# Gate and up as seven block products, 256 tokens moving, outputs through DRAM

## The chip, the core and the metric

The kernel runs on one core of a Trainium2 chip. The metric is device microseconds of one execution; less is better. The engines are TensorE (PE, its weight loads shown apart as PEld), VectorE (DVE), ScalarE (ACT), GpSimd (POOL) and SyncE (SP, which here only issues DMAs).

## The reference, cut to what matters

One decoder block over 512 tokens, D = 2048, in fp32. The change is in its last part, the feed-forward with 5632 hidden columns:

```
u = rmsnorm(h) * (1 + scale2) + shift2                    # 512 x 2048
h = h + gate2 * ((silu(u @ w_gate) * (u @ w_up)) @ w_down)
return rmsnorm(h) * final_norm
```

w_gate and w_up are 2048 x 5632, w_down is 5632 x 2048.

## The kernel before

Activations lie transposed: a tile holds 128 features by 512 tokens. To keep fp32 accuracy at the speed of the fp32r type, every operand is split in a high and a low part (fp32r each) and a product is three matmuls: high*high, low*high, high*low. `mm_ws` (L252 to L255) issues the three with the weights stationary (128x128) and 512 tokens moving; `mm_as` (L257 to L260) does it with activations stationary and up to 288 weight columns moving.

`gemm` walks over the contraction in pairs of 128 rows. For each pair `load_w` brings 128x2x512 weights from DRAM (512 KB, SP queue), ACT casts them to the high part `wh` (L237), DVE subtracts to get the low part `wl` (L238), and PE does 2 x 4 x 3 = 24 matmuls.

The feed-forward runs in four phases over the hidden columns (3, 3, 3 and 2 groups of 512). In a phase each group does a gemm for gate (16 x 4 x 3 = 192 matmuls), SiLU on ACT from PSUM, a gemm for up, the product on DVE (L1045), and the split of the result into `fh`, `fl` (L1048, L1049), which stay in SBUF; then four gemms of `w_down` over the phase's hidden columns, added into `hT` (L999). Over the four phases gate and up are 4224 matmuls and down is 2112, all 512 wide.

Ahead of it the sixteen tiles of `hT` are summed in squares (`sum_rstd`, L819), spread over the partitions (`rows_of`, L171, copied by ACT at L173), and `modulate` makes the sixteen pairs `uh`, `ul` (L384, L386, L390). The last sixth of the adaLN vector is summed on the side (`ada_block`, L356). SP's queue stands in the order in which the code issues; the other engines' order here comes from a scheduler.

## Time and profile before

| | us |
|---|---|
| median of 3 runs | 2519.36 |
| lowest, highest | 2513.86, 2526.12 |
| span of the profiled execution | 2530.7 |
| PE busy in it | 2408.5 (95%) |
| DVE, ACT, POOL busy | 1253.7, 775.3, 231.9 |

Only the profiled execution has a span per instruction; it is 11.3 us longer than the median of the runs that were timed without being shown in detail. Below, a row of a timeline gives start, duration, engine, line, operation, output and inputs; a matmul's duration overlaps the next one's start, so that the pitch is the difference of two starts.

### The profile page before, as it was taken

To read this page: it belongs to the slowest core of one execution; us is meant where nothing else is said; L and a number is where in the kernel's file an instruction comes from. 1 tells how busy PE (TensorE), PEld (TensorE's weight loads), DVE (VectorE), ACT (ScalarE), POOL (GpSimd) and SP (SyncE) were. 2 spreads that over 40 slices of the span, in tenths; PEclk is the share of its full clock that TensorE was granted. 3 is DMA by queue.
4 is the path that set the end of the run, shared out by engine and by line. 5 is a ranking of instruction groups with operands and counts; after the bars stand their busy time and mean duration, and the time that the engine had idled before them with its cause. 6 is when DMAs were issued, how large, how long until landed. Compare 5 with 4: busy or idle time off the path is not lost.

```text
span 2530.7 us, 29434 instructions
## 1 busy us (share of the span) xinstructions
PE 2408.5 (95%) x11475; PEld 2005.5 (79%) x11475; DVE 1253.7 (50%) x1978; ACT 775.3 (31%) x1221; POOL 231.9 (9%) x204
## 2 busy tenths in 40 slices
...
GB/s 301 226 275 77 187 151 125 124 156 114 189 149 150 86 206 226 149 175 191 159 100 92 100 96 96 100 94 97 100 92 100 98 93 100 96 96 100 93 99 100
DMA packets 226794, 339.02 MB, mean 134 GB/s; under 512 B 17648, under 2 KB 102480, under 8 KB 226656
## 3 DMA queue, kind: packets, MB, share of 16 engines
...
q14 instruction: 48, 0.39, 0.1%
...
## 4 chain that ended last, share of the span: by engine, by line
PE 60%; DMA 2%; DVE 1%; issue 0%; ACT 0%; SPq 0%; POOLq 0%; POOL 0%; ACTq 0%; DVEq 0%
PE psmm L253 10%; PE psmm L255 10%; PE psmm L254 10%; PE pss L255 7%; PE pss L253 7%; PE pss L254 7%; PE pso L254 2%; PE pso L253 2%; PE pso L255 2%; DMA wr<-in_w_out_dram 1%; DMA ad<-in_w_ada_dram 1%; DVE acc L356 0%; DVE wl L238 0%; PE psmm L819 0%; ACT wh L237 0%
## 5 line engine op out<-in xcount | busy, mean ns | idle before, releaser
L238 DVE TENSOR_TENSOR wl<-wr,wh 128x1024 fp32r<-128x1024 f32 (+2 forms) x370 | 433.6, 1172 | 966.7 <-ACT wh L237 965.1
L237 ACT CAST wh<-wr 128x1024 fp32r<-128x1024 f32 (+2 forms) x386 | 384.5, 996 | 1199.5 <-PE pso L254 521.7
L253 PE MATMUL psmm<-uh,wh 128*128 128x512 f32 x1010 | 401.0, 398 | 11.9 <-ACT uh L386 5.7
L254 PE MATMUL psmm<-ul,wh 128*128 128x512 f32 x1010 | 398.3, 394 | 2.0 <-DVE ul L390 2.0
L255 PE MATMUL psmm<-uh,wl 128*128 128x512 f32 x1010 | 398.4, 395 | 1.3 <-DVE wl L238 1.3
L253 PE MATMUL pss<-uh,wh 128*128 128x512 f32 x600 | 238.9, 398 | 17.8 <-ACT uh L386 17.8
L254 PE MATMUL pss<-ul,wh 128*128 128x512 f32 x600 | 238.5, 398 | 5.2 <-DVE ul L390 5.2
L255 PE MATMUL pss<-uh,wl 128*128 128x512 f32 x600 | 237.9, 397 | 1.0 <-POOL wl L238 0.9
L253 PEld LDWEIGHTS psmm<-uh,wh 128*128 128x128 f32 x1010 | 192.2, 190 | 54.5 <-ACT uh L386 6.8
L356 DVE SCALAR_TENSOR_TENSOR acc<-ad,sl,acc 128x512 f32<-128x512 f32 x240 | 187.7, 782 | 94.8 <-DMA ad<-in_w_ada_dram 92.2
L255 PEld LDWEIGHTS psmm<-uh,wl 128*128 128x128 f32 x1010 | 192.4, 190 | 43.6 <-DVE wl L238 2.4
L254 PEld LDWEIGHTS psmm<-ul,wh 128*128 128x128 f32 x1010 | 192.2, 190 | 41.7 <-DVE ul L390 3.0
L992 POOL TENSOR_TENSOR fsum<-fsum,sq 128x512 f32<-128x512 f32 x13 | 19.4, 1492 | 1452.7 <-ACT sq L990 1452.0
L253 PEld LDWEIGHTS pss<-uh,wh 128*128 128x128 f32 x600 | 115.3, 192 | 43.9 <-ACT uh L386 19.7
L254 PEld LDWEIGHTS pss<-ul,wh 128*128 128x128 f32 x600 | 115.3, 192 | 31.0 <-DVE ul L390 7.0
L253 PE MATMUL psmm<-fh,wh 128*128 128x512 f32 x352 | 136.9, 389 | 0.0
L254 PE MATMUL psmm<-fl,wh 128*128 128x512 f32 x352 | 136.9, 389 | 0.0
L255 PE MATMUL psmm<-fh,wl 128*128 128x512 f32 x352 | 136.9, 389 | 0.0
L255 PEld LDWEIGHTS pss<-uh,wl 128*128 128x128 f32 x600 | 115.2, 192 | 26.0 <-POOL wl L238 1.8
L492 DVE SCALAR_TENSOR_TENSOR acc<-ad,sl,acc 128x256 f32<-128x256 f32 x144 | 111.2, 772 | 4.8 <-DMA ad<-in_w_ada_dram 0.5
L253 PE MATMUL pss<-fh,wh 128*128 128x512 f32 x264 | 102.7, 389 | 0.0
L254 PE MATMUL pss<-fl,wh 128*128 128x512 f32 x264 | 102.7, 389 | 0.0
...
## 6 DMA issues: line engine op xcount, KB each, us to landing
ad<-in_w_ada_dram SPq DMA_DIRECT2D x192, 512.0 KB, 4.4
wr<-in_w_gate_dram SPq DMA_DIRECT2D x88, 512.0 KB, 3.7
wr<-in_w_up_dram SPq DMA_DIRECT2D x88, 512.0 KB, 3.7
wr<-in_w_down_dram SPq DMA_DIRECT2D x88, 512.0 KB, 3.7
wr<-in_w_in_dram SPq DMA_DIRECT2D x104, 256.0 KB, 3.7
wr<-in_w_in_dram SPq DMA_DIRECT2D x24, 512.0 KB, 4.6
wr<-in_w_out_dram SPq DMA_DIRECT2D x24, 512.0 KB, 4.8
...
```

What stands on the lines that cost most here:

```text
L237: nc.scalar.copy(wh[:, :, s], v)
L238: lo.tensor_tensor(wl[:, :, s], v, split_ap(wh)[:, :, s], op=OP.subtract)
L253: nc.tensor.matmul(dst, wh[:, k, w], ah, start=first, stop=False)
L254: nc.tensor.matmul(dst, wh[:, k, w], al, start=False, stop=False)
L255: nc.tensor.matmul(dst, wl[:, k, w], ah, start=False, stop=last)
L356: nc.vector.scalar_tensor_tensor(acc, wr[:, q, :], s, acc, op0=OP.mult, op1=OP.add)
L492: nc.vector.scalar_tensor_tensor(acc, tiles[n][:, q, :], sc1, acc, op0=OP.mult, op1=OP.add)
L992: nc.gpsimd.tensor_tensor(acc[0], acc[0], sq, op=OP.add)
```

## The change

Gate and up are computed together, as one 2x2 block product: the weights' blocks are (up, gate) by the two halves of the contraction, the activations' blocks are the two halves of the contraction by the two halves of the tokens. The product of 2x2 blocks takes seven block products here (P1 to P7) instead of eight, on sums and differences of blocks that are made beforehand: `w_sums` makes four blocks from the four raw weight blocks, `u_mix` four from the activations. A step s is one 128-row slice of each half for 256 hidden columns: 7 x 2 x 3 = 42 matmuls, the weights stationary, 256 tokens moving. Eight steps make a group of 256 hidden columns; there are 22 groups, 176 steps. Each product has a PSUM bank of its own, out of eight; `evac` adds them up into gate and up, `glu` makes the hidden values, and POOL's queue stores them to DRAM (`hd`), from where `h_tile` reads them again for down.

The low parts of the three blocks that are used unsummed are made by ACT (minus the raw block, rounded to fp32r) and a DMA that adds the raw block onto it (`x_low`, POOL's queue); those of the sums by DVE (`s_split`). `hT` is stored to DRAM after the attention part and read back for down. The order of all engines from the modulation to the first four hidden tiles of down is the code's own (`manual_schedule`). Not shown in the diff: the rope tables move to another pool, `ada_load` and `ada_add` (one 128x256 multiply-add on DVE a step for 128 steps).

```diff
+    fs = ExitStack()
+    ring1 = pool(fs, "ring1", side="right", reuse_waits="tile")
...
+    res = pool(rs, "res", side="right", reuse_waits="tile")
...
+    hT = [res.tile([P, T], F32, name=f"hT{i}") for i in range(ND)]
+    hsd = [dram.tile([P, T], F32, name=f"hsd{i}") for i in range(ND)]
...
+    KG, NG, HT = ND // 2, DFF // 256, T // 2
+    S = KG * NG
+    wg_v = w_gate.rearrange("(h k p) n -> p h k n", h=2, p=P)
+    wu_v = w_up.rearrange("(h k p) n -> p h k n", h=2, p=P)
+    hd = [dram.tile([P, 2, T], F32, name=f"hd{g}") for g in range(NG)]
...
+    def w_load(s):
+        g, k = divmod(s, KG)
+        c = slice(g * HT, (g + 1) * HT)
+        raw[s] = ring1.tile([P, 4, HT], F32, tag="raw", name=uid("raw"), bufs=6)
+        nc.sync.dma_start(raw[s][:, 0:2, :], wu_v[:, :, k, c])
+        nc.sync.dma_start(raw[s][:, 2:4, :], wg_v[:, :, k, c])
+    def w_sums(s):
+        f, t = raw[s], ring1.tile([P, 4, HT], F32, tag="sum", name=uid("sum"), bufs=2)
+        nc.vector.tensor_tensor(t[:, 0:2, :], f[:, 1:3, :], f[:, 0:1, :].to_broadcast([P, 2, HT]), op=OP.add)
+        nc.vector.tensor_tensor(t[:, 2, :], t[:, 0, :], f[:, 2, :], op=OP.add)
+        nc.vector.tensor_tensor(t[:, 3, :], t[:, 2, :], f[:, 3, :], op=OP.add)
+        sums[s] = t
+    def x_high(s):
+        hx[s] = ring1.tile([P, 3, HT], F32R, tag="hx", name=uid("hx"), bufs=3)
+        nc.scalar.copy(hx[s], raw[s][:, 1:4, :])
+    def x_low(s):
+        lx[s] = ring2.tile([P, 3, HT], F32R, tag="lx", name=uid("lx"), bufs=4)
+        nc.scalar.activation(lx[s], raw[s][:, 1:4, :], AF.Copy, scale=-1.0)
+        nc.gpsimd.dma_start(split_ap(lx[s]), raw[s][:, 1:4, :], accum_op=OP.add)
+    def s_split(s):
+        hs[s] = ring2.tile([P, 4, HT], F32R, tag="hs", name=uid("hs"), bufs=2)
+        ls[s] = ring2.tile([P, 4, HT], F32R, tag="ls", name=uid("ls"), bufs=2)
+        nc.scalar.copy(hs[s], sums[s])
+        nc.vector.tensor_tensor(ls[s], sums[s], split_ap(hs[s]), op=OP.subtract)
...
+    def u_raw(k):
+        ur[k] = []
+        for i in (k, k + KG):
+            dst = hT[i] if k < 5 else ev.tile([P, T], F32, tag="ev", name=uid("ur"), bufs=6)
+            nc.vector.scalar_tensor_tensor(dst, hT[i], a_vec[:, 1, i:i + 1], rb, op0=OP.mult, op1=OP.mult)
+            ur[k].append(dst.rearrange("p (a b) -> p a b", b=HT))
+    def u_mix(k, eng):
+        a, b = ur[k]
+        t = ring2.tile([P, 4, HT], F32, tag="tmix", name=uid("tmix"), bufs=2)
+        eng.tensor_tensor(t[:, 0, :], a[:, 1, :], a[:, 0, :], op=OP.subtract)
+        eng.tensor_tensor(t[:, 3, :], b[:, 1, :], t[:, 0, :], op=OP.subtract)
+        eng.tensor_tensor(t[:, 2, :], b[:, 1, :], a[:, 1, :], op=OP.subtract)
+        eng.tensor_tensor(t[:, 1, :], t[:, 3, :], b[:, 0, :], op=OP.subtract)
+        tmix[k] = t
+    def u_split(k):
+        a, b = ur.pop(k)
+        t = tmix.pop(k)
+        h, l = (upool[k // 5].tile([P, 7, HT], F32R, tag="u" + c, name=uid("u" + c), bufs=5 if k < 5 else 3)
+                for c in "hl")
+        sa, sb = (mod[:, 3 * ND + i:3 * ND + i + 1] for i in (k, k + KG))
+        for lo, n, v, sh in ((0, 1, a[:, 0:1, :], sa), (1, 2, b, sb), (3, 2, t[:, 0:2, :], None),
+                            (5, 1, t[:, 2:3, :], dsh[:, k:k + 1]), (6, 1, t[:, 3:4, :], sb)):
+            d = slice(lo, lo + n)
+            if sh is None:
+                nc.scalar.copy(h[:, d, :], v)
+                nc.vector.tensor_tensor(l[:, d, :], v, split_ap(h)[:, d, :], op=OP.subtract)
+            else:
+                nc.scalar.activation(h[:, d, :], v, AF.Identity, bias=sh)
+                nc.vector.scalar_tensor_tensor(l[:, d, :], v, sh, split_ap(h)[:, d, :], op0=OP.add, op1=OP.subtract)
+        V[k] = h, l
+    PROD = (("P1", "x", 1, 0), ("P2", "x", 2, 1), ("P6", "s", 2, 6), ("P7", "s", 1, 5), ("P5", "s", 0, 3),
+            ("P3", "s", 3, 2), ("P4", "x", 0, 4))
+    B = {}
+    def pe(s):
+        g, k = divmod(s, KG)
+        vh, vl = V[k]
+        for name, kind, wi, vi in PROD:
+            if k == 0:
+                B[name] = ps2.tile([P, 2, HT], F32, tag="y", name=uid("py"), bufs=8)
+            wh, wl = (hx[s], lx[s]) if kind == "x" else (hs[s], ls[s])
+            for j in range(2):
+                o, js = B[name][:, j, :], slice(j * P, (j + 1) * P)
+                nc.tensor.matmul(o, wh[:, wi, js], vh[:, vi, :], start=k == 0 and j == 0, stop=False,
+                                 skip_group_check=True)
+                nc.tensor.matmul(o, wh[:, wi, js], vl[:, vi, :], start=False, stop=False, skip_group_check=True)
+                nc.tensor.matmul(o, wl[:, wi, js], vh[:, vi, :], start=False, stop=k == KG - 1,
+                                 skip_group_check=True)
+    def ev_tile():
+        return ev.tile([P, 2, HT], F32, tag="ev", name=uid("ev"), bufs=6)
+    def evac(g):
+        g2, g1, u1, u2 = (ev_tile() for _ in range(4))
+        tt = nc.vector.tensor_tensor
+        nc.scalar.copy(g2, B["P1"])
+        tt(g1, g2, B["P2"], op=OP.add)
+        tt(g2, g2, B["P6"], op=OP.subtract)
+        tt(u1, g2, B["P7"], op=OP.add)
+        tt(g2, g2, B["P5"], op=OP.subtract)
+        tt(u2, B["P5"], u1, op=OP.subtract)
+        tt(g2, g2, B["P3"], op=OP.add)
+        tt(u1, u1, B["P4"], op=OP.add)
+        return g, g1, g2, u1, u2
+    def glu(g, g1, g2, u1, u2):
+        nc.scalar.activation(g1, g1, AF.Silu)
+        nc.scalar.activation(g2, g2, AF.Silu)
+        nc.vector.scalar_tensor_tensor(u1, u1, -1.0, g1, op0=OP.mult, op1=OP.mult)
+        nc.vector.tensor_tensor(u2, u2, g2, op=OP.mult)
+        nc.gpsimd.dma_start(hd[g][:, :, 0:HT], u1)
+        nc.gpsimd.dma_start(hd[g][:, :, HT:], u2)
...
+        for i in range(i0, i0 + n):
+            nc.gpsimd.dma_start(hsd[i], hT[i])
...
+    for s in range(6):
+        w_load(s)
...
-    rb = rows_of(sum_rstd(hsum, D, "mm", "rs2"), "mm", pf.tile([P, T], F32, tag="osum", name="rb2"))
-    u2 = [modulate(1, i, hT[i], rb, pf) for i in range(ND)]
...
+    for s in range(2):
+        w_sums(s)
+    for s in range(2):
+        x_high(s)
+    rb = rows_of(sum_rstd(hsum, D, "mm", "rs2"), "mm", res.tile([P, T], F32, name="rb2"))
+    pk.close()
+    wo.close()
+    aw.close()
...
+    ms.enter_context(tc.manual_schedule())
...
+    ps2 = pool(kk, "ps2", space=bass.MemoryType.PSUM, reuse_waits="tile")
...
+    ev = pool(es, "ev", reuse_waits="tile")
+    ring2 = pool(us, "ring2", reuse_waits="tile")
+    upool = [pool(us, "u0", reuse_waits="tile")]
...
+    def ada_sum(j):
+        b = ps2.tile([P, T], F32, tag="y", name=uid("py"), bufs=8)
+        acc = acc5.pop(j)
+        for i in range(2):
+            nc.tensor.matmul(b[:, i:i + 1], acc[:, i * P:(i + 1) * P], one_col, start=True, stop=True,
...
+        nc.vector.tensor_tensor(mod[:, m0:m0 + 2], b[:, 0:2], b_mod[:, m0:m0 + 2], op=OP.add)
...
+    u_raw(0)
+    u_mix(0, nc.vector)
+    u_raw(1)
+    u_mix(1, nc.gpsimd)
+    for s in range(3):
+        x_low(s)
+    s_split(0)
+    u_split(0)
+    u_raw(2)
...
+    for s in range(S):
+        g, k = divmod(s, KG)
+        if s + 6 < S:
+            w_load(s + 6)
+        if s + 3 < KG:
...
+        if s + 2 < KG:
+            u_mix(s + 2, nc.gpsimd)
+        if s + 1 < KG:
+            u_split(s + 1)
+        if s + 1 < S:
+            s_split(s + 1)
+        if s + 3 < S:
+            x_low(s + 3)
+        if s + 2 < S:
+            x_high(s + 2)
+            w_sums(s + 2)
+        n, i = divmod(s - A0, 4)
+        if 0 <= n < 32 and i == 0:
+            ada_load(n)
+        if 0 < n <= 32:
+            ada_add(n - 1, i)
+        pe(s)
+        if late:
+            late.pop(0)()
+        if k == KG - 1 and s < S - 1:
+            for j in list(acc5):
+                if 4 * (4 * j + 4) + A0 + 3 <= s:
+                    ada_sum(j)
+            e = evac(g)
+            late.append(lambda e=e: glu(*e))
+    us.close()
+    us1.close()
+    fs.close()
...
+    hp = pool(ft, "hp", reuse_waits="tile")
+    hT = [hp.tile([P, T], F32, name=f"hU{i}") for i in range(ND)]
+    wts = pool(ft, "wts2", reuse_waits="tile")
+    pf = pool(ft, "pf2", reuse_waits="tile")
+    phases = [range(0, 12), range(12, 24), range(24, 36), range(36, 44)]
...
-    for ph in phases:
-        a = []
-        for g in ph:
-            G = banks4()
-            gemm([cols(w_gate, 512 * g, 512)], u2, ND, [("ws", m * P, P, G[m]) for m in range(4)], n_ada=1)
...
-                nc.scalar.activation(s, G[m], AF.Silu)
...
-            gemm([cols(w_up, 512 * g, 512)], u2, ND, [("ws", m * P, P, U[m]) for m in range(4)], n_ada=1)
-            for m in range(4):
-                nc.vector.tensor_tensor(sg[m], sg[m], U[m], op=OP.mult)
...
-                nc.scalar.copy(h, sg[m])
-                nc.vector.tensor_tensor(l, sg[m], split_ap(h), op=OP.subtract)
...
+        return [bank(t) for t in (BANKS_B if which[0] else BANKS_A)]
...
+    def h_tile(i):
+        r = pf.tile([P, T], F32, tag="hr", name=uid("hr"), bufs=4)
+        nc.sync.dma_start(r, hd[i // 2][:, i % 2, :])
+        h = pf.tile([P, T], F32R, tag="fh", name=uid("fh"), bufs=24)
+        l = pf.tile([P, T], F32R, tag="fl", name=uid("fl"), bufs=24)
+        nc.scalar.copy(h, r)
+        nc.vector.tensor_tensor(l, r, split_ap(h), op=OP.subtract)
+        return h, l
+    w_first = load_w([cols(w_down, 0, 512)], 0)
+    a = [h_tile(i) for i in range(4)]
+    glu(*evac(NG - 1))
+    ms.close()
+    kk.close()
+    pk = ExitStack()
+    ps = pool(pk, "ps3", space=bass.MemoryType.PSUM, reuse_waits="tile")
+    a += [h_tile(i) for i in range(4, 12)]
+    for p, ph in enumerate(phases):
+        nxt = list(phases[p + 1]) if p < 3 else []
+        b = []
+        nk = len(ph)
         for g in range(4):
             Z = banks4()
-            gemm([cols(w_down[512 * ph[0]:], 512 * g, 512)], a, nk,
-                 [("ws", m * P, P, Z[m]) for m in range(4)])
-            res_add(4 * g, Z, 5, fsum if ph is phases[-1] else None, "fsum")
+            def hook(ct):
+                if p == 0 and ct == 2:
+                    for i in range(4 * g, 4 * g + 4):
+                        nc.sync.dma_start(hT[i], hsd[i])
+                if nxt and (ct % 2 or nk < 12):
+                    b.append(h_tile(nxt.pop(0)))
+            gemm([cols(w_down[P * ph[0]:], 512 * g, 512)], a, nk, [("ws", m * P, P, Z[m]) for m in range(4)],
+                 hook=hook, first=w_first if p == 0 and g == 0 else None)
+            res_add(4 * g, Z, 5, fsum if p == 3 else None, "fsum")
+        a = b
     rf = sum_rstd(fsum, D, "mm", "rs3")
     for i in range(ND):
```

Three places, as the built programs order them. In DVE's order at the start of gate and up (`hT` 8569 to 8584 and before 8563 on are the sixteen residual tiles, `mt` and `ul` the modulated tile and its low part), before:

```order
L384 SCALAR_TENSOR_TENSOR mt_9630<-hT_8563,a_vec,rb_9623 128x512 [waits Activation_49]
L384 SCALAR_TENSOR_TENSOR mt_9636<-hT_8564,a_vec,rb_9623 128x512
L356 SCALAR_TENSOR_TENSOR acc_9736<-ad_9805,sl,acc_9736 128x512 [waits DVE_49]
L390 SCALAR_TENSOR_TENSOR ul_9633<-mt_9630,mod,uh_9632 128x512 [waits Activation_49]
L390 SCALAR_TENSOR_TENSOR ul_9639<-mt_9636,mod,uh_9638 128x512 [waits Activation_49]
```

The first tile's pair is ready after three of these rows. DVE now, from the first block pair's differences on:

```order
L1059 TENSOR_TENSOR tmix_9742<-hT_8569 128x256 [waits DVE_49]
L1060 TENSOR_TENSOR tmix_9742<-hT_8577,tmix_9742 128x256 [waits DVE_49]
L1061 TENSOR_TENSOR tmix_9742<-hT_8577,hT_8569 128x256
L1062 TENSOR_TENSOR tmix_9742<-tmix_9742,hT_8577 128x256 [waits DVE_49]
L1053 SCALAR_TENSOR_TENSOR hT_8570<-hT_8570,a_vec,rb_9715 128x512 [waits DMASW6_49]
L1053 SCALAR_TENSOR_TENSOR hT_8578<-hT_8578,a_vec,rb_9715 128x512 [waits DMASW6_49]
L1045 TENSOR_TENSOR ls_9764<-sum_9680,hs_9763 128x1024
L1079 SCALAR_TENSOR_TENSOR ul_9768<-hT_8569,mod,uh_9767 128x256 [waits Activation_49]
L1079 SCALAR_TENSOR_TENSOR ul_9768<-hT_8577,mod,uh_9767 128x512 [waits Activation_49]
```

Ahead of the first low part of activations now stand the differences, the second block pair's scaling and the low part of the first sums. POOL now, at the same place (`hsd` is the store of `hT`, `lx` the adding DMA of a step's low parts):

```order
L1141 DMA hsd_8600<-hT_8584 128x512 [waits DMASW4_49,DVE_49]
L1059 TENSOR_TENSOR tmix_9749<-hT_8570 128x256 [waits DVE_49,PE_49]
L1060 TENSOR_TENSOR tmix_9749<-hT_8578,tmix_9749 128x256 [waits DVE_49,Pool_49]
L1061 TENSOR_TENSOR tmix_9749<-hT_8578,hT_8570 128x256
L1062 TENSOR_TENSOR tmix_9749<-tmix_9749,hT_8578 128x256 [waits Pool_49]
L1039 DMA lx_9754<-raw_9659 128x768 [waits DMAHW0_49,DMAHW1_49,DMASW5_49,Activation_49]
```

POOL had nothing here before; the first adding DMA now stands behind the second block pair's four differences.

In DVE's order where the up product of a phase is followed by down (`sg` the SiLU of gate, `fl` the hidden tile's low part, `wl` the first low part of `w_down`), before:

```order
L1045 TENSOR_TENSOR sg_11160<-sg_11160,pss_11167 128x512 [waits PE_49]
L1049 TENSOR_TENSOR fl_11412<-sg_11158,fh_11411 128x512 [waits Activation_49]
L1045 TENSOR_TENSOR sg_11162<-sg_11162,pss_11168 128x512 [waits PE_49]
L1049 TENSOR_TENSOR fl_11417<-sg_11160,fh_11416 128x512 [waits Activation_49]
L1045 TENSOR_TENSOR sg_11164<-sg_11164,pso_11169 128x512 [waits PE_49]
L1049 TENSOR_TENSOR fl_11422<-sg_11162,fh_11421 128x512 [waits Activation_49]
L238 TENSOR_TENSOR wl_11467<-wr_11464,wh_11466 128x1024 [waits DMAHW1_49,Activation_49]
```

There the PSUM banks are read first. DVE now, from the last step's low part of sums (`py` 20433 to 20468 are the last group's P2, P6, P7, P5, P3 and P4, `ev` the tiles of `evac`):

```order
L1045 TENSOR_TENSOR ls_20757<-sum_20710,hs_20756 128x1024 [waits PE_49,Activation_49]
L240 TENSOR_TENSOR wl_20876<-wr_20873,wh_20875 128x1024 [waits DMAHW0_49,Activation_49]
L1258 TENSOR_TENSOR fl_20882<-hr_20879,fh_20881 128x512 [waits DMAHW1_49,PE_49,Activation_49]
...
L1109 TENSOR_TENSOR ev_20904<-ev_20903,py_20433 128x512 [waits Activation_49]
L1110 TENSOR_TENSOR ev_20903<-ev_20903,py_20440 128x512 [waits DMASW7_49,DVE_49]
L1111 TENSOR_TENSOR ev_20905<-ev_20903,py_20447 128x512 [waits DVE_49]
L1258 TENSOR_TENSOR fl_20929<-hr_20926,fh_20928 128x512 [waits DMAHW5_49,Activation_49]
L1112 TENSOR_TENSOR ev_20903<-ev_20903,py_20454 128x512 [waits DVE_49]
L1113 TENSOR_TENSOR ev_20906<-py_20454,ev_20905 128x512
L1114 TENSOR_TENSOR ev_20903<-ev_20903,py_20461 128x512 [waits DVE_49]
```

The last group's banks are now read behind the first `wl` of down and four `fl` (three of them left out).

In SP's order at the same place now (`raw` the last weights of gate and up, `hr` hidden tiles from DRAM):

```order
L1023 DMA raw_20481<-in_w_gate_dram 128x2x256 [waits DMAHW7_49]
L223 DMA wr_20873<-in_w_down_dram 128x2x512 [waits DMAHW0_49,DVE_49,PE_49]
L1254 DMA hr_20879<-hd_8601 128x512 [waits DMAHW1_49]
...
L1254 DMA hr_20962<-hd_8606 128x512 [waits DMAHW7_49,DVE_49,Activation_49]
L1254 DMA hr_20968<-hd_8606 128x512 [waits DMAHW0_49,DVE_49,Activation_49]
L223 DMA wr_21002<-in_w_down_dram 128x2x512
```

The first load of `w_down` waits for PE; twelve hidden tiles stand between it and the second.

## Rows read from the trace of the kernel before

**Rows 1.** The page's head and busy times: engine, us (share), instructions.

```profile
span 2530.7 us, 29434 instructions
PE 2408.5 (95%) x11475; PEld 2005.5 (79%) x11475; DVE 1253.7 (50%) x1978; ACT 775.3 (31%) x1221; POOL 231.9 (9%) x204
```

**Rows 2.** Busy times by stretch; the first row names the columns.

```profile
core 0: us, PE busy (x) PEld busy (x) DVE busy (x) ACT busy (x) POOL busy (x), PEclk, DMA share, GB/s
0.00:60.00 60.00, 26.68 (x124) 22.60 (x125) 48.46 (x87) 30.58 (x63) 30.39 (x38) 0.72 0.95 308
1072.00:2509.00 1437.00, 1437.00 (x6356) 1190.19 (x6354) 478.83 (x499) 352.87 (x392) 18.89 (x13) 1.00 0.35 106
1440.00:2420.00 980.00, 980.00 (x4325) 811.49 (x4324) 282.78 (x274) 224.60 (x241) 0.00 (x0) 1.00 0.32 97
```

**Rows 3.** Timeline of PE and PEld: a 256-wide run's ends, two 512-wide, weight loads.

```profile
625.81 0.28 PE L258 MATMUL psmm<-wh,uh 128*128 128x256 f32 x1
...
628.21 0.28 PE L260 MATMUL psmm<-wl,uh 128*128 128x256 f32 x1
...
2421.84 0.39 PE L255 MATMUL pso<-uh,wl 128*128 128x512 f32 x1
2422.07 0.39 PE L253 MATMUL psmm<-fh,wh 128*128 128x512 f32 x1
...
1058.29 1.86 PEld L819 LDWEIGHTS psmm<-cs,sq 128*128 128x128 f32 x16 [0.74 <-ACT sq L990]
```

**Rows 4.** Timeline from the attention output to gate, and down's end.

```profile
1056.46 0.39 PE L255 MATMUL psmm<-yh,wl 128*128 128x512 f32 x1
1061.89 2.08 PE L171 MATMUL psmm<-cs,rs2r 128*128 128x128 f32 x8 [1.66 <-DVE rs2r L165]
1064.06 0.58 ACT L173 COPY rb<-psmm 128x512 f32<-128x512 f32 x1 [3.39 <-PE psmm L171]
1066.24 2.08 PE L253 MATMUL psmm<-uh,wh 128*128 128x512 f32 x4 [2.27 <-ACT uh L386]
...
2508.88 0.39 PE L255 MATMUL pso<-fh,wl 128*128 128x512 f32 x1
```

**Rows 5.** DVE's groups by shape: count | busy us, mean ns | idle before.

```profile
L1049 DVE TENSOR_TENSOR fl<-sg,fh 128x512 fp32r<-128x512 f32 x44 | 30.2, 687 | 0.0
L238 DVE TENSOR_TENSOR wl<-wr,wh 128x1024 fp32r<-128x1024 f32 x262 | 322.2, 1230 | 885.9 <-ACT wh L237 884.5
L578 DVE TENSOR_TENSOR pt<-pss,pt 128x256 fp32r<-128x256 f32 x24 | 10.0, 417 | 2.2 <-ACT pt L577 2.2
L390 DVE SCALAR_TENSOR_TENSOR ul<-mt,mod,uh 128x512 fp32r<-128x512 f32 x16 | 11.4, 744 | 0.3
L390 DVE SCALAR_TENSOR_TENSOR ul<-mt,mod,uh 128x512 fp32r<-128x512 f32 x32 | 29.1, 945 | 0.3
L492 DVE SCALAR_TENSOR_TENSOR acc<-ad,sl,acc 128x256 f32<-128x256 f32 x144 | 111.2, 772 | 4.8 <-DMA ad<-in_w_ada_dram 0.5
```

**Rows 6.** ACT's and POOL's groups by shape, as above.

```profile
L237 ACT CAST wh<-wr 128x1024 fp32r<-128x1024 f32 x262 | 276.2, 1054 | 1014.9 <-PE pso L254 509.1 <-PE psmm L254 454.5 <-issue 39.0
L386 ACT ACTIVATE uh<-mt,mod 128x512 fp32r<-128x512 f32 x16 | 11.0, 720 | 9.4 <-DVE mt L384 9.4
L1048 ACT CAST fh<-sg 128x512 fp32r<-128x512 f32 x44 | 27.3, 620 | 30.0 <-DVE sg L1045 28.9
...
L501 POOL TENSOR_TENSOR acc<-acc,tm 128x256 f32<-128x256 f32 x80 | 68.4, 857 | 83.2 <-ACT tm L500 79.2
L944 POOL DMA_DIRECT2D L<-cumd x8 | 4.0, 507 | 10.0 <-DVE L L940 5.4 <-DVE p L767 4.7
```

**Rows 7.** DMA issues: KB each, median us to landing.

```profile
wr<-in_w_down_dram SPq DMA_DIRECT2D x88, 512.0 KB, 3.7
osp<-o ACTq DMA_DIRECT2D x16, 256.0 KB, 2.9
R<-cumd POOLq DMA_DIRECT2D x8, 4.0 KB, 2.6
```

72 lines of the change are left out of this document (47 added, 25 removed).

## The prediction

> **What bounds the kernel now.** I read the page's head and busy times first [rows 1]: PE is busy for 95% of the span, DVE for half of it. A share over the span hides stages, so next come the busy times by stretch [rows 2]: from 1072 to 2509 us PE is busy without a gap at the full granted clock, 2.4 GHz, while DVE works a third of the time, ACT a quarter and POOL hardly at all. Third the timeline around both ends [rows 4]: the first gate matmul starts at 1066.24, the last down matmul ends at 2509.27. The 6336 matmuls in between have a pitch of 980.00 / 4325 = 0.2266 us [rows 2], together 1435.7; the stretch lasts 1443.0, so only about 7 us are lost, nearly all at the start. Gate and up are 4224 x 0.2266 = 957.1 us of it. Here the time ends on the number of columns that PE moves. Fewer columns are a gain, one for one, as long as nothing else becomes late.
>
> I work out differences on the profiled execution (span 2530.7) and apply their sum to the median, 2519.4, which is 11.3 lower.
>
> **A. The matmuls: -70.** 176 steps of 42 are 7392 matmuls of 256 columns, in place of 4224 of 512: an eighth fewer columns. What a 256-wide one takes, the fused projections show: 20 pitches in 2.40 us, 0.120 each [rows 3], not half of 0.2266 but 0.0067 more. So 7392 x 0.120 = 887.0, a saving of 70.1, of 119.6 if width alone counted. A weight load goes under every matmul: sixteen take 1.86 us, 0.116 each [rows 3], just below the pitch, and the fused projections load anew each time too at 0.120. The pitch therefore stands; a step is 42 x 0.120 = 5.04 us.
>
> The Trainium skill (TensorE: Matmul & The Clock Gate, "LDWEIGHTS") counts 107 ns for a load of 128 columns and would speak against stationary weights under a short moving side; its "Back-to-back issue gap" gives a matmul N/2.4 + 2.5 ns, 109 and 216 ns here, by which the saving would be an estimated 105 us. The trace's 120 and 227 decide: cover is thin, but it holds, and the saving is smaller.
>
> **B. Start: +23, less 6.** Before, one scaling, one high part and one low part stand between `rb` at 1064.64 and the first matmuls [rows 4]. Now two ACT operations of `x_low` come ahead on the path of the norm (some 1.3 us more until `rb`, 1065.9), and DVE has in order: two scalings (2 x 0.744), four differences of 256 (4 x 0.417), two more scalings, the first sums' low part (1.230), the low parts of seven blocks. The last are five operations of 256 or 512, 3 x 0.417 + 2 x 0.744 = 2.74 plus some 0.1 for hand-overs from ACT: 2.86 [rows 5]. They end at 1074.7. POOL makes the second pair's differences (4 x 0.857 = 3.43 [rows 6]) from 1070.6 on, and behind these issues the first adding DMA (0.51 [rows 6]; landing 2.6 to 3.7 [rows 7]), so that the product with `lx`, the third matmul, starts at about 1077.5. From there the first group goes at DVE's pace: 1.49 + 2.86 + 1.23 + `w_sums` 1.52 (0.687 + 2 x 0.417) = 7.10 us a step, for five steps; 5.61 for two; both above 5.04. The group ends at 1125.0 if POOL's differences don't stretch DVE. They do: the same scaling has a mean of 0.945 over 32, of which 16 at 0.744 had no POOL work beside them [rows 5], so 1.146 for the others, 0.40 more each; for the 24 differences it is 1134.6. I take the middle, 1130, against 1066.2 + 8 x 5.04 = 1106.6: **+23.4**, bounds +11.2 (the lag of the third matmul alone) and +31.5. The 6.4 us that the old start loses at the cold clock and between tiles are already within this: **-6.4**.
>
> The Trainium skill (SBUF — State Buffer, "Who interferes with whom") has a DVE instruction with two SBUF inputs contend with a POOL instruction that reads SBUF. The rows 0.744 and 0.945 agree.
>
> **The steady step: 0.** Against PE's 5.04 us: DVE `w_sums` 1.52, `ls` 1.23, the adaLN multiply-add 0.42 to 0.77, a share of `evac` and `glu` (nine operations, 6.2 / 8 = 0.78), 4.0 to 4.3. ACT casts 1024 (1.054), 768 twice (between 0.620 and 1.054 each) and a little, 3.0. POOL issues one DMA, 0.51. The transfers move 524 KB of weights, 131 KB of adaLN and 64 KB of hidden values, 721 KB; at 97 GB/s by a share of 0.32, 303 GB/s [rows 2], 2.38 us. The adding DMA's 393 KB is the one price that no row shows. Its bounds by plain transfers: 1.30 us if it goes at their rate, 3.9 if reading the addend, reading the target and writing each cost a pass. The nearest rows are plain DMAs with a pass; an add has to do more, so I take two, 2.6, whereby the 16 engines are at 4.98 of 5.04. That is tight, and it is the case's largest risk (rival 1). Each `lx` is issued about two steps ahead, some 10 us, against landings of 2.6 to 3.7 [rows 7]; this covers a transfer three times slower, not a full queue.
>
> **C. Group ends: +9.** Seven of eight PSUM banks hold the products. P1's bank is copied by ACT first, then DVE reads them in the order in which PE needs them again; 0.687 per operation [rows 5] against 6 x 0.120 = 0.72 per product: just in time, 0. In eight of the 22 groups `ada_sum` takes the spare bank and puts an addition that waits for PE ahead of `evac` on DVE; I put 1.15 us on each (two loads and two matmuls at 0.12, the addition at no more than 0.417, and 0.25 for hand-overs), 9.2. Bounds 0 and 20, the latter if all 22 ends lose 0.9.
>
> **D. From up to down: +17.** Before, PE goes from the last up matmul to the first down matmul with a pitch of 0.23 [rows 3]: no gap, because the next weights were there. Now the first `w_down` load waits for PE's last use of a buffer of `ls` (its place is taken), 0.72 us before the end of gate and up. Then: landing 3.7 [rows 7], cast 1.05, `wl` 1.23, four `fl` 2.75, three `evac` operations, one more `fl`, three more `evac` operations, as DVE's order has them; the first down matmul needs a bank that these free. 3.7 + 1.05 + 1.23 + 2.75 + 7 x 0.687 = 13.5, less 0.72: PE stands for 12.8. The second load of `w_down` stands on SP behind twelve tiles of hidden values, eight of them waiting for a buffer: issue at about 18, landing at 21.8, cast by 22.9. PE, started at 12.8, has worked 24 matmuls, 5.44 us, and waits again; the second pair starts at 22.9 rather than 5.44 + 0.7, so the stage is **16.7** late. Bounds 10 (hidden tiles land early) and 24 (tiles from DRAM behind their stores).
>
> Costed at nothing: the stores of `hT`, 16 x 256 KB on POOL's queue under the attention output's matmuls, and the early weight loads there (the DMA share is 0.32 to 0.35 in the later stages [rows 2]; if that cover is gone, a landing of 3.7 at most); the reads of `hT` and of hidden tiles during down (DVE 1.23 + 0.69 per 5.44 us). The end of the kernel is unchanged.
>
> **Sum:** -70.1 - 6.4 + 23.4 + 9.2 + 16.7 = -27.2, so 2492 us. All kind bounds at once (+11.2, 0, +10) give -55, 2464; all unkind ones (+31.5, +20, +24) -1, 2518. Taking some of each: 2472 to 2512.
>
> **Rivals.**
>
> (1) *The adding DMAs make DMA the bound: slower.* Place: the steady step, 176 times. It decides from 2.66 us per add (5.04 - 2.38), and has eaten the whole net gain at 2.66 + 27 / 176 = 2.82. At the three-pass price, 3.9, a step takes 6.28 and the kernel 2492 + 176 x 1.24 = 2710; at 3.2, 2587. For it: the room is tight by my own middle value, and a DMA share of 0.95 at 308 GB/s, in the first 60 us [rows 2], shows that there is no more rate. Against: the adaLN and the stores end before the last groups, and the 3 KB runs per partition are long.
>
> The Trainium skill (Collectives: The Full Stack, "The bandwidth ceiling: the fold count and why AG ≠ RS ≠ AR") states that an add in a DMA costs two source reads, hence about half the rate; an estimate by it is 2.6 us, which just fits. No row here shows it.
>
> (2) *DVE becomes the bound: slower.* If transfers or POOL's DMA work stretch DVE as the multiply-add beside POOL was (0.772 against 0.417 for a plain 256 one, 1.85 times [rows 5]), its step is 1.85 x (1.52 + 1.23 + 0.42) + 0.78 = 6.64 us, 1.6 over PE's, 176 times: 2774. It decides from a stretch of 1.34, and at 1.4 gives 2492 + 176 x 0.18 = 2524. Against: DVE's 1.230 and 0.687 were measured with DMAs running.
>
> (3) *Only the matmuls count: faster still.* No stretch at the start, no loss at group ends, a short change to down: -50 to -65, 2455 to 2470.
>
> (4) *The gain is eaten:* unkind bounds everywhere and a pitch of 0.123 (+22): 2512 to 2560.
>
> **How the numbers follow.** The forecast (net gain, 2472 to 2512) 0.62; (3) 0.10; (4) 0.07; (1) 0.16, of which some 0.03 ends below 2570; (2) 0.05. About 0.5%, 12.6 us, is what a measurement of this kernel can tell from no change. Faster by more than that, below 2507: 0.56 + 0.10 = 0.66. Within it: 0.06 of the forecast and 0.05 of (4) = 0.11. Slower: 0.02 + 0.16 + 0.05 = 0.23. The range that leaves 2 in 10 out takes the forecast, (3), (4) and the near end of (1): 2455 to 2570.
>
> **What would show it.** A: a pitch of 0.120 in the second half of gate and up, 5.04 us a step. B: third matmul near 1077, end of the first group near 1130, POOL's differences at 0.86. C: gaps of about a microsecond at those group ends that have adaLN sums, none at the others. D: no matmul for some 13 us after the last product, and a second gap of about 4. Rival 1: a DMA share near 1 from 1200 to 1900, `lx` landing later from step to step, PE waiting for `lx`. Rival 2: `ls` and `w_sums` well over 1.23 and 1.52, PE waiting for `hs`/`ls`. The prediction is wrong if a step in the middle of gate and up is not 5.04 us.

## The result and the profile after

The changed kernel takes 2495.9 us (median of 4 runs, 2492.28 to 2498.48) against 2522.74 beside it: a ratio of 0.9898, 95% interval 0.9874 to 0.9922. That is 26.8 us less; the prediction had 27.2 less, 2492. Page of the changed kernel, head and busy times, to be held against [rows 1]:

```profile
span 2490.4 us, 38618 instructions
PE 2336.9 (94%) x14643; PEld 2094.0 (84%) x14643; DVE 1633.2 (66%) x2757; ACT 1055.0 (42%) x1619; POOL 458.1 (18%) x468
```

PE is busy 72 us less, DVE 380 us more. The busy times by stretch (columns as in [rows 2]) show the first group of gate and up, its middle, the change to down, and down:

```profile
1060.00:1120.00 60.00, 45.19 (x334) 42.57 (x334) 58.33 (x80) 34.77 (x56) 39.62 (x37) 0.91 0.61 139
1200.00:1800.00 600.00, 600.00 (x5027) 598.97 (x5026) 448.03 (x738) 323.90 (x401) 124.45 (x149) 1.00 0.90 222
1968.00:1995.00 27.00, 10.33 (x35) 7.91 (x34) 16.12 (x24) 12.42 (x19) 1.46 (x2) 0.70 0.72 241
1995.00:2468.00 473.00, 473.00 (x2085) 391.42 (x2083) 171.70 (x180) 126.37 (x146) 19.12 (x13) 1.00 0.36 119
```

In the middle PE is as full as before, at 2.4 GHz; in the first row it is DVE that is full (58.33 of 60), and in the third nobody is. The timeline of PE gives the places: the first three products with what each waited for, and two matmuls of the last step that are 39 starts apart.

```profile
1054.58 0.58 PE L1096 MATMUL py<-uh,hx 128*128 128x256 f32 x1 [2.00 <-ACT uh L1078]
1059.48 0.58 PE L1098 MATMUL py<-ul,hx 128*128 128x256 f32 x1 [4.33 <-DVE ul L1079]
1066.32 0.58 PE L1099 MATMUL py<-uh,lx 128*128 128x256 f32 x1 [6.25 <-DMA lx<-raw]
...
1963.72 0.28 PE L1099 MATMUL py<-uh,lx 128*128 128x256 f32 x1
...
1968.36 0.28 PE L1099 MATMUL py<-uh,lx 128*128 128x256 f32 x1
```

4.64 / 39 = 0.119 a matmul; a group of 336 takes 40.05 us (table below), so 0.1192 a matmul and 5.01 a step. PE's waits between the attention output and down, from the view of waits (engine, line, who ended the wait; us in total, times, longest):

```profile
PE pss L255 <- DVE ev L1114: 12.7, 1, 12.7
PE py L1098 <- DVE ul L1079: 9.9, 8, 4.3
PE py L1099 <- DMA lx<-raw: 6.2, 1, 6.2
PE pss L255 <- ACT wh L239: 4.0, 1, 4.0
PE py L1099 <- DVE ls L1045: 3.0, 4, 0.8
```

The table is worked out from the starts of the matmuls in each timeline, in us from the end of the attention output on. (Ahead of it the code hardly differs, and executions scatter: the output ends at 1045.3 to 1056.3 us in the profiles of the changed kernel and of its variants, at 1056.7 in that of the kernel before. That is why the two profiled spans differ by 40 us and the medians by 27.)

| kernel | first product | end of 1st group | a group, 4th to 19th | 20th to 22nd | end of products to last down matmul | whole |
|---|---|---|---|---|---|---|
| before | 9.6 | - | - | - | - | 1474.0 |
| changed | 8.8 | 74.5 | 40.37 | 40.05 | 499.5 | 1444.7 |
| e1 no add | 8.3 | 73.3 | 40.37 | 40.05 | 500.1 | 1442.6 |
| e3 low parts by DVE | 8.3 | 82.4 | 42.93 | 41.93 | 501.6 | 1502.2 |
| e12 the same, first in order | 8.3 | 81.2 | 40.57 | 40.05 | 501.1 | 1455.1 |
| e4 differences by DVE | 8.8 | 71.2 | 40.37 | 40.05 | 500.9 | 1442.2 |
| e8 start | 10.0 | 68.6 | 40.37 | 40.05 | 493.1 | 1431.6 |
| e5 224 KB more | 9.1 | 74.7 | 40.37 | 40.05 | 499.7 | 1443.6 |
| e11 512 KB more | 8.9 | 74.4 | 41.08 | 40.05 | 500.1 | 1456.2 |
| e6 banks first | 9.5 | 75.1 | 40.37 | 40.05 | 496.4 | 1441.9 |
| e7 change to down | 8.9 | 74.4 | 40.37 | 40.05 | 497.2 | 1440.8 |
| e9 tiles of down early | 8.3 | 73.9 | 40.37 | 40.05 | 480.5 | 1423.5 |
| e10 both | 9.9 | 68.5 | 40.37 | 40.05 | 480.5 | 1418.1 |

### The profile page after: what moved, and what is told of

The parts are those of the page before. It is cut to its first block, busy times and chain, and to the rows that moved or that the text cites. A ratio compares the mean times of both kernels' runs of the same rounds, so it can differ in the third digit from the quotient of the medians.

```text
span 2490.4 us, 38618 instructions
## 1 busy us (share of the span) xinstructions
PE 2336.9 (94%) x14643; PEld 2094.0 (84%) x14643; DVE 1633.2 (66%) x2757; ACT 1055.0 (42%) x1619; POOL 458.1 (18%) x468
## 4 chain that ended last, share of the span: by engine, by line
PE 53%; DVE 1%; DMA 1%; ACT 0%; issue 0%; POOLq 0%; POOL 0%; SPq 0%; DVEq 0%; ACTq 0%
PE py L1096 11%; PE py L1099 11%; PE py L1098 11%; PE psmm L256 3%; PE psmm L257 3%; PE psmm L255 3%; PE pss L255 2%; PE pss L256 2%; PE pss L257 2%; PE pso L256 1%; PE pso L257 1%; PE pso L255 1%; DMA wr<-in_w_down_dram 0%; DMA out_dram<-ot 0%; DVE ot L1297 0%
## 5 line engine op out<-in xcount | busy, mean ns | idle before, releaser
L1099 PE MATMUL py<-uh,ls 128*128 128x256 f32 x1408 | 398.4, 283 | 3.0 <-DVE ls L1045 3.0
L1098 PE MATMUL py<-ul,hs 128*128 128x256 f32 x1408 | 399.0, 283 | 1.5 <-DVE ul L1079 1.5
L1096 PE MATMUL py<-uh,hs 128*128 128x256 f32 x1408 | 399.5, 284 | 1.0 <-DVE ev L1113 0.5
L1045 DVE TENSOR_TENSOR ls<-sum,hs 128x1024 fp32r<-128x1024 f32 x176 | 215.3, 1224 | 195.3 <-ACT hs L1044 195.3
L1098 PE MATMUL py<-ul,hx 128*128 128x256 f32 x1056 | 297.4, 282 | 8.3 <-DVE ul L1079 8.3
L1099 PE MATMUL py<-uh,lx 128*128 128x256 f32 x1056 | 298.0, 282 | 6.2 <-DMA lx<-raw 6.2
L1096 PE MATMUL py<-uh,hx 128*128 128x256 f32 x1056 | 299.3, 283 | 2.3 <-ACT uh L1078 2.0
L1099 PEld LDWEIGHTS py<-uh,ls 128*128 128x128 f32 x1408 | 269.0, 191 | 4.0 <-DVE ls L1045 3.8
L1096 PEld LDWEIGHTS py<-uh,hs 128*128 128x128 f32 x1408 | 268.3, 191 | 2.6 <-issue 0.7
L1098 PEld LDWEIGHTS py<-ul,hs 128*128 128x128 f32 x1408 | 268.4, 191 | 2.3 <-DVE ul L1079 2.3
```

Source lines behind the costliest of these rows:

```text
L1045: nc.vector.tensor_tensor(ls[s], sums[s], split_ap(hs[s]), op=OP.subtract)
L1096: nc.tensor.matmul(o, wh[:, wi, js], vh[:, vi, :], start=k == 0 and j == 0, stop=False, skip_group_check=True)
L1098: nc.tensor.matmul(o, wh[:, wi, js], vl[:, vi, :], start=False, stop=False, skip_group_check=True)
L1099: nc.tensor.matmul(o, wl[:, wi, js], vh[:, vi, :], start=False, stop=k == KG - 1, skip_group_check=True)
```

## The experiments

### What the adding DMAs cost (e1, e5, e11)

e1 leaves the add out:

```diff
-        nc.gpsimd.dma_start(split_ap(lx[s]), raw[s][:, 1:4, :], accum_op=OP.add)
```

> The adding DMA of the low parts is left out (the tile keeps minus the raw block; the result is not the block's output). Theory A, the adding DMAs are hidden beside PE and the start goes at DVE's pace: a step stays at 5.01 us, the DMA share between 1200 and 1800 us falls from 0.90 to about 0.48, by which an add costs (0.90 - 0.48) x 5.01 = 2.1 us, and the first group still ends some 74 us after the attention output; the time is that of the changed kernel, 2496, or up to 2 us less. Theory B, the adds crowd the queues: the groups that also load adaLN go from 40.36 to 40.05 us (-5 in all) and the 6.25 us that PE waits for the first low part come back whole: 2485.

Measured: 2491.89 us (2486.19 to 2497.37), ratio 0.9883 (0.9863 to 0.9904). The stretch in the middle, columns as above:

```profile
1200.00:1800.00 600.00, 600.00 (x5026) 598.98 (x5025) 447.63 (x737) 323.83 (x401) 21.09 (x30) 1.00 0.45 144
```

The share falls from 0.90 to 0.45: by this measure an add takes 0.45 x 5.01 = 2.25 us of the engines, 1.7 times the 1.30 that the prediction had for a plain pass (e5 below shows that the share is no measure of what is used up). The groups are as long as with it, to 0.01 us; theory A. The third product comes 4 us earlier, yet the first group ends only 1.2 us earlier: the wait of 6.2 us for the first low part is the longest of the start in the view of waits, and removing it gains next to nothing, because DVE is late behind it anyway (PE's waits for `ul` and `ls`, 9.9 + 3.0 us in the changed kernel, are 12.2 + 4.0 in e1).

The Trainium skill (Collectives: The Full Stack, "The bandwidth ceiling: the fold count and why AG ≠ RS ≠ AR") has an add read two sources, at about half the rate. The 1.7 here, a ratio of shares, agrees in kind.

How much room is left? e5 adds a load that nobody reads, on SP's queue, and e11 in the same place a copy of 512 KB from DRAM to DRAM (e2, a load of 256 KB, found no room in SBUF and has no result); e5:

```diff
+        if s >= 16:
+            z = ring1.tile([P, 2, 224], F32, tag="z", name=uid("z"), bufs=1)
+            nc.sync.dma_start(z, wg_v[:, :, k, g * HT:g * HT + 224])
```

> One more load of 224 KB a step from step 16 on, into a tile that nobody reads. Theory A, the 16 DMA engines have 0.5 us a step left in the steps that load adaLN (share 0.90 of 5.01): 229 KB at 303 GB/s are 0.76 us, so that such a step takes about 5.27, +0.26 in some 125 steps, +32 us on the changed kernel, near 2527 (2510 to 2540); the steps without adaLN stay at 5.01. Theory B, the share is no measure of what is left: the time stays at 2495, within 4 us.

> In e5 a step moved 1340 KB in 5.01 us with the DMA share at 1.01 and cost nothing. Here 512 KB more a step than in the changed kernel, copied from DRAM to DRAM: 1640 KB. Theory A, the rate has a ceiling near the highest that was seen, 308 GB/s: 5.32 us a step with adaLN, +0.3 in 125 steps, +39 us in all, and the first weights and low parts land late. Theory B, no ceiling there yet: steps stay at 5.01 (327 GB/s) and the time is that of the changed kernel.

e5 took 2502.22 us against 2525.68 of the kernel before beside it, ratio 0.9906 (0.9891 to 0.9921; the changed kernel 0.9898), so no measurable cost: B. e11, one run: 2510.25 us. Their middles and, under e11's, its issues (KB each, us to landing), then the same two of the changed kernel:

```profile
1200.00:1800.00 600.00, 600.00 (x5026) 598.97 (x5025) 448.26 (x737) 324.29 (x402) 124.31 (x149) 1.00 1.01 268
```

```profile
1200.00:1800.00 600.00, 593.48 (x4939) 590.93 (x4938) 441.98 (x727) 320.09 (x395) 122.58 (x147) 1.00 1.07 316
...
lx<-raw POOLq DMA_DIRECT2D x176, 384.0 KB, 7.5
raw<-in_w_up_dram SPq DMA_DIRECT2D x176, 256.0 KB, 10.8
```

```profile
lx<-raw POOLq DMA_DIRECT2D x176, 384.0 KB, 4.9
raw<-in_w_up_dram SPq DMA_DIRECT2D x176, 256.0 KB, 4.1
```

At a share of 1.01 the groups are as long as without the load (40.37 and 40.05). A share that passes 1 and costs nothing is no fraction of what the engines can do; that the time of packets under way contains their waiting for each other would explain it, and is not measured by itself. In e11, at 316 GB/s, groups get longer, 40.37 to 41.08 in the mean, far less than theory A's 0.3 a step, with landings of the weights at 10.8 in place of 4.1. The loss is not even: the groups from the 4th to the 19th take 40.15 to 44.54 us. There ACT stands for the weights (167 us in 79 waits from 1200 to 1880 us; in the changed kernel none of ACT's waits there is for a DMA), and the longest of PE's waits are for ACT's copy of P1's bank (4.7 us in 7). So what e11 shows are late landings, not a ceiling of the rate; the changed kernel itself moves 378 GB/s from 1996 to 2000 us. At 222 GB/s in its middle it has at least 46 GB/s to spare; where between 268 and 316 the loss begins stays open.

### Are the adding DMAs needed (e3, e12)

```diff
-        nc.scalar.activation(lx[s], raw[s][:, 1:4, :], AF.Copy, scale=-1.0)
-        nc.gpsimd.dma_start(split_ap(lx[s]), raw[s][:, 1:4, :], accum_op=OP.add)
+        nc.vector.tensor_tensor(lx[s], raw[s][:, 1:4, :], split_ap(hx[s]), op=OP.subtract)
```

with `x_low(s + 1)` behind `s_split(s + 1)` in e3, ahead of it in e12.

> The low parts of the three unsummed blocks are made by DVE (raw minus high part), as those of the sums are; no adding DMA, no negation on ACT. DVE has 3.74 us a step in the middle (448 of 600) and gets 0.92 more (768 of 1024 columns at 1.22). Theory A: 4.66 still fits under 5.01, so that the middle stays; the start, which goes at DVE's pace, gets 0.92 a step longer for six steps, about +5: 2501 (2497 to 2506). Theory B: at group ends, where six reads of PSUM and two products are added, DVE falls behind and PE waits for banks, 1 us or more in each of 21: 2520 or more.

e3 took 2550.7 us, ratio 1.0111 (1.0092 to 1.0131): slower than the kernel before, by more than theory B said. Its waits from 1130 to 1960 us (the changed kernel has none in that view):

```profile
PE py L1098 <- DVE lx L1038: 24.6, 20, 1.3
PE py L1185 <- DVE acc L1179: 6.3, 8, 0.8
PE py L1095 <- DVE ev L1112: 5.1, 12, 0.5
```

And the timelines of DVE and PE of e3, in an ordinary step and then behind a group's end:

```profile
1938.98 1.22 DVE L1044 TENSOR_TENSOR ls<-sum,hs 128x1024 fp32r<-128x1024 f32 x1 [1.19 <-ACT hs L1043]
...
1951.47 0.68 DVE L1114 TENSOR_TENSOR ev<-ev,py 128x512 f32<-128x512 f32 x1
1952.07 1.22 DVE L1044 TENSOR_TENSOR ls<-sum,hs 128x1024 fp32r<-128x1024 f32 x1
1953.20 0.95 DVE L1038 TENSOR_TENSOR lx<-raw,hx 128x768 fp32r<-128x768 f32 x1
...
1954.21 0.39 PE L1098 MATMUL py<-uh,lx 128*128 128x256 f32 x1 [1.21 <-DVE lx L1038]
```

PE needs `lx` first and `ls` 1.4 us later; DVE makes them the other way round behind seven reads of banks, and in the ordinary step it stands 1.19 us until ACT has made `hs` from the sums that DVE has just finished. Is it work or order?

> e3 with one exchange in DVE's order: the low part of the unsummed blocks is made before that of the sums, where DVE stands 1.19 us for the high part from ACT, and in the order in which PE needs them. In e3 a group in the middle takes 1.9 to 2.6 us longer than in the changed kernel; PE waits for that low part behind the reads of the banks. Theory A, e3 lost by order: the 1.2 us wait per group goes, the groups end 0.5 to 1 us long, 2551 - 22 x 1.2 = 2524. Theory B, e3 lost by the amount of work between two groups (6.2 us of bank reads and products beside 4.2 to 4.7 a step): then the wait moves to the low part of the sums and the time stays near 2550.

e12: 2510.97 us, ratio 0.9926 (0.9900 to 0.9952), better than theory A's 2524. The groups without adaLN are back at 40.05, those with it at 40.57, and of the 57 us of e3 over the changed kernel 47 were order alone. What is left, 10.4 us from the attention output on, is what the adding DMAs are worth against this order of DVE: 6.7 at the end of the first group, 3 in the groups with adaLN.

### What sets the pace of the start (e4, e8)

e4: `u_mix(..., nc.vector)` in place of `nc.gpsimd`.

> The differences of the activations' blocks are all made by DVE, none by POOL. In the changed kernel a step of the first group takes 8.25 us on DVE, 1.55 more than its operations take where POOL is idle. Theory A, POOL's operations stretch those of DVE: the stretch goes and four operations of 0.42 come, 6.7 + 1.67 = 8.4 a step; the time is that of the changed kernel within 3 us. Theory B, the stretch comes from the transfers and stays: 8.25 + 1.67 = 9.9 a step, six times, +9: 2505.

2492.16 us, ratio 0.9883 (0.9868 to 0.9898). DVE's groups by shape between 1075 and 1105 us in the changed kernel, then between 1080 and 1110 in e4 (count, busy us, mean ns):

```profile
L1053 DVE SCALAR_TENSOR_TENSOR ur<-hT,a_vec,rb 128x512 f32<-128x512 f32 x6 | 7.1, 1224 | 0.0
L1028 DVE TENSOR_TENSOR sum<-sum,raw 128x256 f32<-128x256 f32 x3 | 2.5, 847 | 0.1
```

```profile
L1053 DVE SCALAR_TENSOR_TENSOR ur<-hT,a_vec,rb 128x512 f32<-128x512 f32 x6 | 4.2, 745 | 0.0
L1028 DVE TENSOR_TENSOR sum<-sum,raw 128x256 f32<-128x256 f32 x4 | 1.7, 426 | 0.1
```

With POOL's differences gone, 1224 becomes 745 and 847 becomes 426, while the transfers went on: the stretch was POOL's, theory A. The step of the first group is read from the same matmul in two steps that follow each other, here in the changed kernel:

```profile
1085.04 0.39 PE L1098 MATMUL py<-ul,hx 128*128 128x256 f32 x1 [1.34 <-DVE ul L1079]
1093.29 0.39 PE L1098 MATMUL py<-ul,hx 128*128 128x256 f32 x1 [1.34 <-DVE ul L1079]
```

That is 8.25 us; in e4 the same matmul starts at 1086.25 and 1094.15, 7.90, though DVE has four operations more. POOL's help costs DVE more than it saves it.

e8 takes this and puts DVE's work that needs no norm ahead of it:

```diff
+    for s in range(3):
+        x_low(s)
+    for s in range(2):
+        s_split(s)
+    w_sums(2)
     u_raw(0)
     u_mix(0, nc.vector)
...
```

> All differences of activations by DVE (as in e4) and, besides, the low parts of the first two sums and the third step's sums made while DVE waits for the norm, not after it. Theory A, the first group goes at DVE's pace and only DVE's work after the norm counts: 2 x 1.2 + 1.5 us go, of which about 1.2 us is work that still lies after the norm; the first group ends 67 to 69 us after the attention output, in place of 71.2 in e4 and 74.5 in the changed kernel: 2490. Theory B, the first low part of the weights (landing of the adding DMA) decides, which this does not touch: 71, 2492.

2491.36 us, ratio 0.9865 (0.9850 to 0.9879). The first group ends at 68.6, as theory A said: of the 6 us against the changed kernel 3.3 are e4's and 2.7 the new order. The other gain was not foreseen: down begins 7.3 us after the last product in place of 12.9, and the stretch to its end is 493.1 in place of 500.9 in e4. Since `lx`, `hs` and `ls` are now the first tiles of their pool, they lie where later `hT` comes, and the first weights of down lie on the adaLN tiles, which were long done with: their load issues at 1931.58, 40 us before the last product, where the changed kernel's issues 0.4 us before it. Nothing of down's code was touched; the order of allocation in a pool 900 us earlier was.

### The change to down (e6, e7, e9, e10)

The changed kernel's timeline of all engines there:

```profile
1967.96 0.37 SPq L223 DMA_DIRECT2D wr<-in_w_down_dram  x1
1968.37 16.82 SPq L1254 DMA_DIRECT2D hr<-hd  x12
1972.05 1.04 ACT L239 CAST wh<-wr 128x1024 fp32r<-128x1024 f32 x1 [13.13 <-DMA wr<-in_w_down_dram]
1973.13 1.23 DVE L240 TENSOR_TENSOR wl<-wr,wh 128x1024 fp32r<-128x1024 f32 x1 [12.95 <-ACT wh L239]
1974.27 2.49 DVE L1258 TENSOR_TENSOR fl<-hr,fh 128x512 fp32r<-128x512 f32 x4
1976.68 0.68 DVE L1109 TENSOR_TENSOR ev<-ev,py 128x512 f32<-128x512 f32 x1
1980.52 0.68 DVE L1114 TENSOR_TENSOR ev<-ev,py 128x512 f32<-128x512 f32 x1
1981.34 0.77 PE L255 MATMUL pss<-fh,wh 128*128 128x512 f32 x1 [12.70 <-DVE ev L1114]
1985.24 0.50 SPq L223 DMA_DIRECT2D wr<-in_w_down_dram  x1
1993.08 0.79 PE L255 MATMUL pss<-fh,wh 128*128 128x512 f32 x1 [3.97 <-ACT wh L239]
```

The first load of the weights issues 0.4 us before the last matmul (1968.36, above), the second one 17.3 us later, behind twelve hidden tiles. e6 moves `glu(*evac(NG - 1))` ahead of the first weights and tiles.

> The last group's banks are read (and its hidden values made) before the first weights and hidden tiles of down are split. The changed kernel waits 12.7 us for the banks there and 4.0 for the second weights. Theory A, the second load of the weights decides, which stands behind twelve hidden tiles on SP: the first wait falls to about 4.7 (until the first high part of the weights), the second grows to about 10, so that the end of down comes some 4 us earlier. Theory B, the wait named in the trace is the cost: the whole 8 us between bank and weights come back.

One run, 2497.26 us. The waits:

```profile
PE pss L255 <- ACT wh L239: 6.8, 1, 6.8
PE pss L255 <- ACT fh L1257: 5.5, 1, 5.5
```

12.3 us in place of 16.7: 7 us of the first wait go, 2.8 come back on the second. Theory A, in its mechanism: what the first wait gives up returns in part on the second (6.8 us where A had about 10), and down ends 3.1 us earlier behind the products, where A had 4.

e7 loads more weights before the hidden tiles, puts the weights' pool first and lets down begin on other banks:

```diff
+    wts = pool(ft, "wts2", reuse_waits="tile")
     hp = pool(ft, "hp", reuse_waits="tile")
...
-    wts = pool(ft, "wts2", reuse_waits="tile")
...
-    w_first = load_w([cols(w_down, 0, 512)], 0)
-    a = [h_tile(i) for i in range(4)]
-    glu(*evac(NG - 1))
+    f0, f1, f2 = [fetch_w([cols(w_down, 0, 512)], ct) for ct in range(3)]
+    hr = [h_load(i) for i in range(4)]
+    w_first = [f0()]
+    a = [h_tile(i, hr[i]) for i in range(2)]
+    e = evac(NG - 1)
+    w_first.append(f1())
+    a += [h_tile(i, hr[i]) for i in range(2, 4)]
...
```

> The change to down made anew: the weights' tiles of down lie where the adaLN tiles were (free long before), three loads of weights go ahead of the hidden tiles on SP, wl and two fl are made before the banks are read, and the first group of down takes the banks of P2, P6, P7 and P5, which are read first. Theory A, that the 12.8 and 4.0 us are queue order and place alone: from the last product to the last down matmul it takes 480 to 484 us in place of 499.5, and the time is 2478 (2475 to 2483). Theory B, what is late next is DVE, which has some 9 us of work in this place whatever the order (banks, two products, wl twice, four fl): half of it comes back, 2487.

2499.27 us, ratio 0.9896 (0.9879 to 0.9912): no gain that can be measured, and both theories missed. Its ACT and PE:

```profile
1979.19 1.04 ACT L239 CAST wh<-wr 128x1024 fp32r<-128x1024 f32 x1 [9.76 <-PE py L1100]
1985.61 1.27 ACT L1262 CAST fh<-hr 128x512 fp32r<-128x512 f32 x2 [5.37 <-DMA hr<-hd]
...
1988.34 0.77 PE L255 MATMUL psmm<-fh,wh 128*128 128x512 f32 x1 [9.19 <-DVE ev L1110]
```

The first weights were there, but their high part was to be written on memory that PE still read: the cast waited 9.76 us for `py`, the end of the products. So did the second load, and the hidden tiles behind it. e9 keeps the loads and banks of e7, but both weights and four hidden tiles are split ahead of the reads of the banks, and all of it lies where the first five activation pairs were (`pq` takes the tiles of the last norm's sums and fills the place between):

```diff
     hp = pool(ft, "hp", reuse_waits="tile")
...
+    pq = pool(ft, "pq", reuse_waits="tile")
     wts = pool(ft, "wts2", reuse_waits="tile")
...
-        h = pf.tile([P, T], F32R, tag="fh", name=uid("fh"), bufs=24)
-        l = pf.tile([P, T], F32R, tag="fl", name=uid("fl"), bufs=24)
...
+        hl = pf.tile([P, 2, T], F32R, tag="fhl", name=uid("fhl"), bufs=24)
+        h, l = hl[:, 0, :], hl[:, 1, :]
...
+    a = [h_tile(i, hr[i]) for i in range(4)]
+    w_first += [f1(), f2]
     glu(*evac(NG - 1))
...
```

> The change to down once more. In e7 the first high part of the weights, the second load and the low parts of the hidden tiles lay on memory that PE reads until its last product, so that they began only at 1979.19, and PE went on waiting, 9.2 us. Here weights, hidden tiles and their parts lie where the first five pairs of activations were, which PE is done with three steps earlier; three loads of weights and four hidden tiles come ahead; both wl and four fl are made before the banks are read. Theory A, place and queue order were the whole cost: PE waits under 1 us at the end of gate and up and from the last product to the last down matmul it takes 479 to 483 us (499.5 in the changed kernel, 497.2 in e7); ratio to the kernel before about 0.983. Theory B, DVE's work in this place (5.2 us ahead of the banks' 4.8) is late next: 487 to 491.

2480.12 us, ratio 0.9823 (0.9807 to 0.9840). DVE and PE at the end of the products, 1977.83:

```profile
1970.58 2.49 DVE L1266 TENSOR_TENSOR fhl<-hr,fhl 128x512 fp32r<-128x512 f32 x4
1972.99 1.22 DVE L240 TENSOR_TENSOR wl<-wr,wh 128x1024 fp32r<-128x1024 f32 x1
1975.74 0.68 DVE L1113 TENSOR_TENSOR ev<-ev,py 128x512 f32<-128x512 f32 x1
...
1977.83 0.40 PE L255 MATMUL psmm<-fhl,wh 128*128 128x512 f32 x1
...
1980.67 0.50 PE L255 MATMUL psmm<-fhl,wh 128*128 128x512 f32 x1 [1.29 <-DVE ev L1118]
```

PE goes over without a gap; 1.29 us for one bank is all that is left. Theory A: 480.5 against 499.5.

> The start of e8 and the change to down of e9 together. They lie 900 us apart and share no wait: from the attention output to the end 1444.7 - 6 - 18 = about 1421 us, ratio to the kernel before about 0.980. If the order of the pools in e8 (which alone brought the first load of down 6 us forward) were what e9 does, the gains would not add: 1425 to 1431.

e10, e8 and e9 together: 2472.3 us (2468.24 to 2477.71), ratio 0.9793 (0.9772 to 0.9815), 1418.1 from the attention output on: the gain at the start (first group at 68.5) and that at the change to down (480.5) add; what e8 gained at down is contained in e9's. It is the fastest of all these kernels, with the reference's computation unchanged.

## Why the prediction was right, and where its terms were not

From the attention output to the end the two profiles differ by 1474.0 - 1444.7 = 29.3 us. By the terms of the prediction:

| term | predicted | measured | from |
|---|---|---|---|
| A matmuls | -70.1 | -76.0 | 957.1 to 22 x 40.05 = 881.1 |
| what the old stretch lost | -6.4 | -7.3 | 1443.0 - 1435.7 |
| B start | +23.4 | +27.1 | 74.5 - 8.8 - 40.05 = 25.6; first product 0.7 earlier; 2.2 in the second group |
| C group ends | +9.2 | +5.1 | 16 x (40.37 - 40.05) |
| D up to down | +16.7 | +20.9 | 499.5 - 2112 x 0.2266 |
| end of the kernel | 0 | +1.0 | 22.4 against 21.4 |
| sum | -27.2 | -29.2 | |

The total owes much of its closeness to luck: the errors of the terms, 5.9, 0.9, 4.1 on one side and 3.7, 4.2, 1.0 on the other, nearly cancel.

- **A.** The mechanism held: width alone would have given 119.6, the 256-wide pitch decided, and the weight loads stayed under it. The pitch was 0.1192 (40.05 / 336), not 0.120; on 7392 matmuls that is 5.9 us. The run of twenty fixes its own mean to about 0.0005, so the 0.0008 is a difference between the two kinds of product; its cause stays open.
- **B.** Right in its mechanism, DVE's pace, shown by e1 (the DMA wait removed, 1.2 us gained), e4 (POOL's stretch of DVE removed, 3.3) and e8 (DVE's work moved ahead of the norm, 2.7 more). The step was 8.25, where I had 7.10 and a stretch on top. The size of the stretch was read wrongly: the 1.146 for an operation beside POOL is a mean over sixteen, and in the trace of the kernel before nine of these take 1.21 to 1.23 us, six 0.75 and one 2.88; 1.22 is what the scalings of the first group take now. POOL's differences, put at 0.86, take 0.79 to 1.19, and the first of each four 1.64 to 2.25. Two figures of the working don't follow from its terms: 1077.5 + 5 x 7.10 + 2 x 5.61 is 1124.2 and not 1125.0, and of the bound +31.5 only 28.0 is worked out. Missed: DVE is still behind when the first banks are to be read, so that the second group is 42.21 long.
- **C.** I put 1.15 us on each of the eight adaLN sums; it is 0.64 (5.1 / 8), spread over two groups. Where the sum's matmuls stand, two products' starts are 0.49 apart (1242.40 and 1242.89) in place of 0.12; the rest is lost at three matmuls of the group behind. That the addition stands ahead of `evac` on DVE makes the first bank read start 0.6 us after the last product (1243.14) and not 1.4 before it, as in the group without a sum that ends at 1202.47. The rest of the loss may come from this; that is not shown.
- **D.** The two waits were foreseen at 12.8 and about 4 and measured 12.7 and 4.0, in the order of queues that the prediction spelled out. Most of the missing 4.2 is the clock: behind each wait PE works at a granted clock of 0.50, that is 1.2 GHz, before it is back at 1.00 (columns as in [rows 2]):

```profile
1981.34:1985.30 3.96, 3.96 (x9) 3.12 (x10) 3.96 (x7) 1.31 (x3) 1.46 (x2) 0.50 0.40 135
1985.80:1988.80 3.00, 3.00 (x15) 2.40 (x13) 0.68 (x2) 0.62 (x1) 0.00 (x0) 1.00 0.93 288
```

  The ten pitches from 1981.34 to 1985.75 take 4.4 us in place of 2.3, and the seven from 1993.08 to 1996.13 3.05 in place of 1.6: 3.6 together. In e9, where PE stands for 1.29 us and no longer, the granted clock is 1.00 from 1977 to 1990. I had costed the wait and not what follows it.
- **The end of the kernel** was put at no change; its 1.0 us lies within the scatter of the changed kernel's variants (20.8 to 22.4 us behind the last down matmul).
- **Rival 1** did not come: the add is 2.25 us by share, near my 2.6, but the point from which I let it decide was wrong. I divided bytes by a rate of 303 GB/s, which is bytes over share in a stretch with a share of 0.32, and took the 308 GB/s of [rows 2] for the most there is; 316 GB/s cost only 0.7 us a group (e11). The chance I gave to it was too high for the reason I gave.
- **Rival 2** did not come either: DVE is stretched only where POOL computes, in the first group. The Trainium skill (SBUF — State Buffer, "Who interferes with whom") names the pair, DVE with two SBUF inputs beside POOL; 1224 against 745 ns agrees.
